# Expert products of a transformer layer: 256 weight columns per matmul in place of 512

## The chip, the core and the metric

The kernel runs on one core of a Trainium2 chip. The metric is the device time of one execution in microseconds (us); less is better. The core has a matmul engine (PE, with its weight loads shown apart as PEld), three engines for elementwise work (DVE, ACT, POOL), a queue engine (SP), and 16 DMA engines. On PE one operand is stationary: a load (LDWEIGHTS) puts it into the array, and a matmul then streams the moving operand past it, column by column, into PSUM. The next load may run while a matmul streams.

## What is computed

A layer with three attention branches (differential attention, RWKV-7 time mixing, memory attention), a joint output projection, and a mixture of 16 experts, all in f32. 512 tokens of width 1024; each token goes to 2 of 16 experts of hidden width 512. The part that the change touches is the last loop:

```python
y = jnp.zeros_like(xt)
for e in range(N_EXPERTS):
    hdn = jax.nn.silu(xt @ w_gate[e]) * (xt @ w_up[e])
    y = y + gate[:, e:e + 1].astype(xt.dtype) * (hdn @ w_down[e])
return y.reshape(B, S, D)
```

## The kernel before

Each expert gets a table of up to 96 token slots (`CAP`). Its rows are gathered from memory (`gather`), turned on PE against an identity (`turn_x`), and split into a high and a low part (`xh`, `xl`, f32r). The expert's weights stream in by pieces of 128 partitions x 1024 columns, 512 KB each, 12 pieces an expert (4 of gate, 4 of up, 4 of down), issued by SP. For each piece `WeightStream.pump` makes a high part on ACT (`whi`, L96) and a low part on DVE (`wlo`, L97); there are four pairs of these tiles, and a pair comes free (`ws.cool`) when the products that read it have run.

A product keeps f32 accuracy with three matmuls (`mm3`, L242 to L245): high x high, high x low, low x high. In an expert the activations are the stationary operand (128 partitions x 96 columns) and the weights are the moving one (128 x 512). `in_product` (gate, then up) runs 8 slices of the contraction x 3 matmuls into one PSUM bank (`pp`); `down` runs 4 slices x 2 halves of the output x 3 matmuls into two banks (`py`; for the last expert two `pp`). That is 24 + 24 + 24 = 72 matmuls an expert and 1152 in all. Between the products of an expert stand the turns of the next expert's rows (`turn_x`, L1280, 8 matmuls) and of the hidden rows (`turn_h`, L1302, 4 matmuls), and the table of a later expert (`table`, L1223, 4 small matmuls).

The order of the instructions on each engine is made ahead of the run by a scheduler that has its own estimate of what each takes. So a change in the form of the matmuls can move others around them, on all engines.

Two earlier stages use matmuls of 256 moving columns, with 128 stationary columns: the projections (mm3 on `w_in` and `w_kv`) and the output projection (`out_part`, L998 to L1000):

```python
T.matmul(o, ah, hi[:, k % 4, :], start=k == k0 and i == lead, stop=False, skip_group_check=True)
T.matmul(o, ah, lo[:, k % 4, :], start=False, stop=False, skip_group_check=True)
T.matmul(o, al, hi[:, k % 4, :], start=False, stop=k == k1, skip_group_check=True)
```

Of the kernel before, what the change touches and what calls it, by code (L numbers as in the profile page):

```python
# [24 lines left out]
KC = D // P  # L25
# [3 lines left out]
CAP = 96  # L29
# [121 lines left out]
def hybrid_layer_kernel(ctx, tc, x, mem, positions, cols, w_in, w_kv, w_out, wa2, g2, ffn, wr, br,  # L151
                        wg, wu, wd, out):
    nc = tc.nc
    V, A, G, T = nc.vector, nc.scalar, nc.gpsimd, nc.tensor
# [16 lines left out]
    def pp():  # L171
        return psp.tile([P, 512], F32, name="pp", bufs=4)
# [69 lines left out]
    def mm3(ps, ah, al, bh, bl, first, last):  # L242
        T.matmul(ps, ah, bh, start=first, stop=False)  # L243
        T.matmul(ps, ah, bl, start=False, stop=False)  # L244
        T.matmul(ps, al, bh, start=False, stop=last)  # L245

    def paired(steps):

        before = steps[0]()
        for step in steps[1:]:  # L250
            with tc.issue_after(before.ins):
                before = step()

    def rsqrt(pool, ss, n, mul, epsv, tag, wide=False):
        v = pool.tile([P, n], F32, name="rs_v" + tag)
        y = pool.tile([P, n], F32, name="rs_y" + tag)
        t = pool.tile([P, n], F32, name="rs_t" + tag)
        V.tensor_scalar(v, ss, mul, epsv, op0=ALU.mult, op1=ALU.add)
        if wide:
            G.tensor_tensor(y, v, mhalf.to_broadcast([P, n]), op=ALU.pow)  # L260
        else:
            A.activation(t, v, AF.Ln)
            A.activation(y, t, AF.Exp, scale=-0.5)
        V.tensor_mul(t, y, y)
        V.scalar_tensor_tensor(t, t, -0.5, v, op0=ALU.mult, op1=ALU.mult)
        V.scalar_tensor_tensor(y, t, 1.5, y, op0=ALU.add, op1=ALU.mult)
        return y
# [256 lines left out]
    def rwkv():  # L524
# [4 lines left out]
        with tc.manual_schedule(engines={mybir.EngineType.Activation}):  # L529
            A.activation(th[0:64, :], lor[0:64, 0, :], AF.Tanh)  # L530
            A.activation(th[64:128, :], lor[64:128, 0, :], AF.Copy)
            A.activation(sg, lor[:, 1, :], AF.Sigmoid)
            yield 1.8
            f0 = b4("f0", [P, 4 * S + 2 * NCH])
            f1 = bR("f1", [P, 2, 2, S])
            f2 = bR("f2", [P, 2, 2, S])
            pc_ = f0[:, 0:2 * S + 2 * NCH].rearrange("p (j c t) -> p j c t", j=2, t=C + 1)
            sw = f0[:, 2 * S + 2 * NCH:].rearrange("p (j t) -> p j t", j=2)
            cs, kk, sq, ip = f1[:, 1], f2[:, 0], f2[:, 1], f1[:, 1]
            aa = f1[:, 0]  # L540
            V.memset(pc_[:, :, :, 0], 1.0)
            for j in range(2):
                pw = [pc() for _ in range(2)]
                paired([lambda o=o: T.matmul(pw[o], wa2_sb[sr(o), j * P:(j + 1) * P], th[sr(o), :], start=True, stop=True)
                        for o in range(2)])
                for dst, nb, ps in ((sw, 0, pw[0]), (aa, 2, pw[1])):
                    A.activation(dst[:, j, :], ps, AF.Sigmoid, bias=col[:, C_W0 + nb + j:C_W0 + nb + j + 1])
                V.tensor_tensor_scan(cs[:, j, :], rmask, sw[:, j, :], 0.0, op0=ALU.mult, op1=ALU.add)
                yield 2.0
            A.preload_act_table_set("natural_log_exp_and_others")  # L550
            A.activation(pc_[:, :, :, 1:], cs.rearrange("p j (c t) -> p j c t", t=C), AF.Exp, scale=-KAPPA)
            A.activation(ip, cs, AF.Exp, scale=KAPPA)
# [59 lines left out]
        for ci in range(4):  # L612
            pq = [pc() for _ in range(2)]
            paired([lambda h=h, q=q: T.matmul(pq[q][:, h * P:(h + 1) * P], bk[sr(q), ci, h], u1[sr(q), q, ci, h],
                                              start=True, stop=True) for h in range(4) for q in range(2)])
            for q in range(2):
                pv = pq[q].rearrange("p (h n) -> p h n", h=4)
                A.activation(u2[sr(q), ci, :, 0:64], pv[sr(q), :, 0:64], AF.Copy)
                V.tensor_mul(u2[sr(q), ci, :, 64:128], pv[sr(q), :, 64:128],
                             gm[sr(q), None, 64:128].to_broadcast([64, 4, 64]))  # L620
                V.tensor_mul(u1[vr(q), q, ci], pv[vr(q)], gm[vr(q), None, :].to_broadcast([64, 4, P]))
                yield 1.0
# [79 lines left out]
        def inverse(q):  # L702
            ra = slice(q * 64, q * 64 + 32)
            rb = slice(q * 64 + 32, q * 64 + 64)
            ps = pc()
            for i in range(16):
                T.matmul(ps[rb, i * 32:(i + 1) * 32], u2v[ra, i, 32:64], zt[ra, i, 0:32], start=True, stop=True)
            A.activation(qt[rb].rearrange("p u n -> p (u n)"), ps[rb, :], AF.Copy)
            yield 2.0
            ps = pc()  # L710
            for i in range(16):
                T.matmul(ps[rb, i * 32:(i + 1) * 32], u2v[rb, i, 32:64], qt[rb, i, :], start=True, stop=True)
            A.activation(zt[rb, :, 0:32], ps[rb, :].rearrange("p (u n) -> p u n", n=32), AF.Copy)
            yield 2.0
            for g in range(2):
                ps = pc()
                ps2 = pc()

                def merge(i, second):
                    ci, h = divmod(g * 8 + i, 4)  # L720
                    zl = zt[sr(q), g * 8 + i, :]
                    if second:
                        return T.matmul(ps2[vr(q), i * C:(i + 1) * C], zl, u2[sr(q), ci, h, 64:128], start=True, stop=True)
                    return T.matmul(ps[sr(q), i * C:(i + 1) * C], zl, bkt[sr(q), q * 4 + ci, h, :], start=True, stop=True)
                paired([lambda i=i, z=z: merge(i, z) for i in range(8) for z in (False, True)])
                A.activation(bkt[sr(q), q * 4 + g * 2:q * 4 + g * 2 + 2].rearrange("p c h n -> p (c h) n"),
                             ps[sr(q), :].rearrange("p (u n) -> p u n", n=C), AF.Copy)
                A.activation(u2v[sr(q), g * 8:g * 8 + 8, 64:128], ps2[vr(q), :].rearrange("p (u n) -> p u n", n=C),
                             AF.Copy)
                yield 2.0  # L730
# [301 lines left out]
    def pl(n):  # L1032
        return pools["ps"].tile([P, 96], F32, name="pl", bufs=2)[:, 0:n]
# [139 lines left out]
    def step(t, n=1):  # L1173
        for _ in range(n):
            next(turns[t])
# [107 lines left out]
    def in_product(xh, xl):  # L1283
        ps = pp()
        for b in range(4):
            hi, lo = ws.use()
            for k in range(2):
                kk_ = b * 2 + k
                mm3(ps[0:CAP, :], xh[:, kk_, :], xl[:, kk_, :], hi[:, k, :], lo[:, k, :], kk_ == 0, kk_ == KC - 1)
            ws.cool(1)  # L1290
        return ps

# [21 lines left out]
    def down(hh, hl, si, gs, last=False):  # L1314
        py = [pp(), pp()] if last else pools["ps"].tile([P, 2, 512], F32, name="py", bufs=1)
        for k in range(4):
            hi, lo = ws.use()
            for n in range(2):
                ns = slice(n * 512, (n + 1) * 512)
                mm3(py[n][0:CAP, :] if last else py[0:CAP, n, :], hh[:, k, :], hl[:, k, :], hi[:, 0, ns], lo[:, 0, ns], k == 0, k == 3)  # L1320
            ws.cool(1)
        ye = ex_p.tile([CAP, D], F32, name="ye", bufs=3)
        if last:
            A.activation(ye[:, 0:512], py[0][0:CAP, :], AF.Copy, scale=gs)
            V.tensor_scalar(ye[:, 512:D], py[1][0:CAP, :], gs, None, op0=ALU.mult)
        else:
            A.activation(ye, py[0:CAP].rearrange("p a b -> p (a b)"), AF.Copy, scale=gs)
        G.indirect_dma_start(out, bass.IndirectOffsetOnAxis(ap=si, axis=0), ye, None, compute_op=ALU.add)  # L1328
# [17 lines left out]
    for e in range(NE):  # L1346
        pg = in_product(*xt_)
        if e + LEAD < NE and e + LEAD > 3:
            with tc.issue_after(last_x[-1].ins):
                table(e + LEAD, e + LEAD + 1)()  # L1350
            xg.append(gather(gidx[0:CAP, e + LEAD:e + LEAD + 1]))
        hs = turn_h(sl) if sl is not None else None
        xt2 = turn_x(xg[e + 1]) if e + 1 < NE else None
        pu = in_product(*xt_)
        sl = hidden(pg, pu)
        xt_ = xt2
        if hs:
            down(*hs, sidx[0:CAP, e - 1:e], gslot[0:CAP, e - 1:e])
# [12 lines left out]
    with tc.If(full > CAP):  # L1371
        with tc.For_i(0, NE, 1) as e:
# [5 lines left out]
            for b in range(1, (S + CAP - 1) // CAP):  # L1378
                base = ex_p.tile([P, CAP], F32, name="base")
                V.tensor_scalar(base, slot1, float(b * CAP), None, op0=ALU.add)  # L1380
                ps = pl(96)
# [56 lines left out]
```

## Time and profile before

| what | us |
|---|---|
| time, median of 3 runs (lowest, highest) | 634.29 (633.48, 638.74) |
| the profiled execution: its time | 633.17 |
| its span from first to last instruction | 631.4 |
| PE busy in the span | 600.7 |
| DVE, ACT, POOL busy | 498.0, 413.0, 126.3 |
| expert stage, about | from 335 to 619 |

The profile shows one execution. A matmul's duration in it is a model that holds its pipeline too, so that durations of matmuls that follow each other overlap; what a matmul costs in a dense stretch is the step from its start to the start of the next. The same is true of loads. Some matmul records are missing from the trace (3986 of 4021 are there).

### The profile page before, as it was taken

Reading aid. Unit: us, or ns where it says so; the run is one execution under the profiler, and the core shown is the slowest. Engines: PE = TensorE matmul, PEld = TensorE weight load, DVE = VectorE, ACT = ScalarE, POOL = GpSimd, SP = SyncE. Lnnn points to the kernel's source line nnn. Section 1 sums busy time; section 2 is a strip of 40 time slices with the busy share of each in tenths; the row PEclk is TensorE's granted clock in tenths of the full one; section 3 lists DMA queues with packets and bytes.
Section 4 is the critical chain, followed back from the end, with each engine's and each line's share of the span. In section 5 each row is a group of like instructions: output and inputs, shape, how many; then the busy total and the mean of one; then the engine's idle time right before and its main releaser. Section 6 shows DMA issues by size and latency. Waiting matters only on the chain.

```text
span 631.4 us, 10888 instructions
## 1 busy us (share of the span) xinstructions
PE 600.7 (95%) x3986; PEld 482.1 (76%) x3986; DVE 498.0 (79%) x893; ACT 413.0 (65%) x622; POOL 126.3 (20%) x129
## 2 busy tenths in 40 slices
PE   3899999999999999999998999999999999999992
PEld 3777879999998877889996777777777777777771
DVE  5854996699755778555468999999999999988991
ACT  3677344544367766655247788888889888888880
POOL 6802010335400114304001011111011111310001
PEclk9999989999999999999999999999999999999997
DMA  8523233333432030889789999999999999799813
GB/s 304 158 79 87 80 102 83 101 95 108 103 83 68 2 134 1 292 278 344 274 315 310 354 348 370 369 372 356 360 357 363 364 366 373 227 379 374 320 25 54
DMA packets 77501, 144.17 MB, mean 228 GB/s; under 512 B 12832, under 2 KB 30496, under 8 KB 77440
## 3 DMA queue, kind: packets, MB, share of 16 engines
q1 hardware_dynamic: 69200, 126.07, 56.9%
q0 software_dynamic: 3760, 13.24, 8.9%
q10 hardware_dynamic: 4480, 4.09, 2.1%
q8 instruction: 33, 0.54, 0.4%
q14 instruction: 28, 0.23, 0.1%
HBM read 131.72 MB, written 11.67 MB: 227 GB/s over the span
## 4 chain that ended last, share of the span: by engine, by line
PE 86%; DVE 6%; ACT 3%; DMA 2%; issue 1%; POOL 1%; POOLq 0%; ACTq 0%; DVEq 0%
PE pp L243 16%; PE pp L245 16%; PE pp L244 16%; PE py L244 5%; PE py L245 4%; PE py L243 4%; PE pp L998 2%; PE pp L999 2%; PE pp L1000 2%; PE pt L921 2%; PE pp L1280 1%; PE py L1136 1%; PE pc L781 1%; DVE wlo L97 1%; PE pl L1103 1%
## 5 line engine op out<-in xcount | busy, mean ns | idle before, releaser
L245 PE MATMUL pp<-whi,xl 128*96 128x512 f32 x264 | 104.0, 395 | 0.0
L244 PE MATMUL pp<-wlo,xh 128*96 128x512 f32 x264 | 103.8, 394 | 0.0
L243 PE MATMUL pp<-whi,xh 128*96 128x512 f32 x264 | 101.2, 394 | 0.8 <-ACT xh L1267 0.8
L1328 POOL DMA_INDIRECT out<-ye,sidx x16 | 23.2, 1452 | 226.0 <-DVE gidx L1230 90.7
L97 DVE TENSOR_TENSOR wlo<-raw,whi 128x1024 fp32r<-128x1024 f32 x42 | 52.3, 1258 | 15.5 <-ACT whi L96 15.0
L96 ACT ACTIVATE whi<-raw 128x1024 fp32r<-128x1024 f32 x42 | 44.1, 1059 | 31.2 <-PE pp L245 14.0
L243 PE MATMUL pp<-whi,hm_h 128*128 128x256 f32 x224 | 63.5, 284 | 0.1
L245 PE MATMUL pp<-whi,hm_l 128*128 128x256 f32 x224 | 63.3, 283 | 0.0
L244 PE MATMUL pp<-wlo,hm_h 128*128 128x256 f32 x224 | 63.1, 282 | 0.0
L243 PEld LDWEIGHTS pp<-whi,xh 128*96 128x96 f32 x264 | 42.5, 161 | 19.6 <-ACT xh L1267 1.3
L245 PEld LDWEIGHTS pp<-whi,xl 128*96 128x96 f32 x264 | 42.6, 161 | 18.4
L244 PEld LDWEIGHTS pp<-wlo,xh 128*96 128x96 f32 x264 | 42.5, 161 | 18.2
L244 PE MATMUL py<-wlo,hh 128*96 128x512 f32 x120 | 47.9, 399 | 0.0
L245 PE MATMUL py<-whi,hl 128*96 128x512 f32 x120 | 47.1, 392 | 0.0
L243 PE MATMUL py<-whi,hh 128*96 128x512 f32 x120 | 47.0, 392 | 0.0
L97 DVE TENSOR_TENSOR wlo<-u,whi 128x1024 fp32r<-128x1024 f32 x34 | 40.8, 1224 | 6.3 <-ACT whi L96 6.3
L97 DVE TENSOR_TENSOR wlo<-lraw,whi 128x1024 fp32r<-128x1024 f32 x36 | 42.6, 1218 | 2.8 <-ACT whi L96 2.7
L243 PEld LDWEIGHTS pp<-whi,hm_h 128*128 128x128 f32 x224 | 42.0, 188 | 2.0 <-issue 0.7
L245 PEld LDWEIGHTS pp<-whi,hm_l 128*128 128x128 f32 x224 | 42.1, 188 | 0.6 <-issue 0.2
L244 PEld LDWEIGHTS pp<-wlo,hm_h 128*128 128x128 f32 x224 | 42.1, 188 | 0.5 <-issue 0.2
L96 ACT ACTIVATE whi<-lraw 128x1024 fp32r<-128x1024 f32 x36 | 37.1, 1059 | 5.1 <-PE pp L245 3.6
L96 ACT ACTIVATE whi<-u 128x1024 fp32r<-128x1024 f32 x34 | 35.2, 1058 | 6.7 <-PE pp L1000 3.7
(397 smaller groups left out, 1545.5 us busy)
## 6 DMA issues: line engine op xcount, KB each, us to landing
raw<-in_w_in SPq DMA_DIRECT2D x22, 512.0 KB, 3.8
u<-in_wd SPq DMA_DIRECT2D x12, 512.0 KB, 7.3
lraw<-in_wg SPq DMA_DIRECT2D x12, 512.0 KB, 11.7
lraw<-in_wu SPq DMA_DIRECT2D x12, 512.0 KB, 9.3
lraw<-in_wd SPq DMA_DIRECT2D x12, 512.0 KB, 12.5
f<-in_wg SPq DMA_DIRECT2D x11, 512.0 KB, 10.3
u<-in_wu SPq DMA_DIRECT2D x11, 512.0 KB, 12.5
eraw<-in_wd SPq DMA_DIRECT2D x10, 512.0 KB, 13.4
```

The costliest lines, as they stand in the source:

```text
L96: nc.scalar.activation(hi, slot, AF.Copy)
L97: nc.vector.tensor_sub(lo, slot, hi.bitcast(F32))
L243: T.matmul(ps, ah, bh, start=first, stop=False)
L244: T.matmul(ps, ah, bl, start=False, stop=False)
L245: T.matmul(ps, al, bh, start=False, stop=last)
L781: T.matmul(px[:, h * C:(h + 1) * C], u1[:, q, ci, h], sav[:, c, h, :], start=h == 0, stop=True, skip_group_check=True)
L921: T.matmul(po[:, 0:P], aws[i % 2][:, kb * P:(kb + 1) * P], qk["v"][:, kb, h * P:(h + 1) * P], start=kb == 0, stop=kb == qb)
L998: T.matmul(o, ah, hi[:, k % 4, :], start=k == k0 and i == lead, stop=False, skip_group_check=True)
L999: T.matmul(o, ah, lo[:, k % 4, :], start=False, stop=False, skip_group_check=True)
L1000: T.matmul(o, al, hi[:, k % 4, :], start=False, stop=k == k1, skip_group_check=True)
L1103: T.matmul(pr_[:, 0:20], xT[:, k, :], wr_sb[:, k, :], start=k == 0, stop=k == KC - 1)
L1328: G.indirect_dma_start(out, bass.IndirectOffsetOnAxis(ap=si, axis=0), ye, None, compute_op=ALU.add)
```

## The change

The three matmuls of a slice become six: each is cut into two with half of the moving columns (256), into the two halves of the same PSUM bank. The stationary operand of both is the same. In the first slice only the first of the six has the start flag.

```diff
+    def mm3_halves(ps, ah, al, bh, bl, first, last):
+        for z, (a, b) in enumerate(((ah, bh), (ah, bl), (al, bh))):
+            for n in range(2):
+                c = slice(n * 256, n * 256 + 256)
+                T.matmul(ps[:, c], a, b[:, c], start=first and z + n == 0, stop=last and z == 2, skip_group_check=True)
...
-                mm3(ps[0:CAP, :], xh[:, kk_, :], xl[:, kk_, :], hi[:, k, :], lo[:, k, :], kk_ == 0, kk_ == KC - 1)
+                mm3_halves(ps[0:CAP, :], xh[:, kk_, :], xl[:, kk_, :], hi[:, k, :], lo[:, k, :], kk_ == 0, kk_ == KC - 1)
...
-                mm3(py[n][0:CAP, :] if last else py[0:CAP, n, :], hh[:, k, :], hl[:, k, :], hi[:, 0, ns], lo[:, 0, ns], k == 0, k == 3)
+                mm3_halves(py[n][0:CAP, :] if last else py[0:CAP, n, :], hh[:, k, :], hl[:, k, :], hi[:, 0, ns], lo[:, 0, ns], k == 0, k == 3)
```

Lines behind the new function stand 6 further down in the kernel after: L1302 is L1308 there, and the matmuls of L243 to L245 are at L258.

PE, in the middle of an expert, before: the last slice of a down product (`py`) begins, one product of the next matrix (`pp`) follows, then the turns (L1302, L1280) and the four matmuls of a table (L1223, with their loads), and the down product goes on.

```order
L243 MATMUL py_4686<-whi3_87,hh_4626 96x512
L243 MATMUL pp_4726<-whi0_80,xh_4640 96x512
L1302 MATMUL pp_4783<-ident_104,sl_4683 128x96 x4
L1280 MATMUL pp_4792<-ident_104,xg_4457 128x96 x4
L1280 MATMUL pp_4793<-ident_104,xg_4457 128x96 x4
L1223 LDWEIGHTS ohs_4764
L1223 MATMUL pl_4763<-rhs_3188,ohs_4764 96x6
...
L1223 LDWEIGHTS ohs_4773
L1223 MATMUL pl_4763<-rhs_3188,ohs_4773 96x6
L244 MATMUL py_4686<-wlo3_88,hh_4626 96x512
```

The same place after:

```order
L258 MATMUL py_5070<-whi3_87,hh_4986 96x256 x2
L258 MATMUL pp_5134<-whi0_80,xh_5000 96x256 x2
L1308 MATMUL pp_5215<-ident_104,sl_5067 128x96 x4
L1286 MATMUL pp_5224<-ident_104,xg_4745 128x96 x4
L1229 LDWEIGHTS ohs_5196
...
L1286 MATMUL pp_5225<-ident_104,xg_4745 128x96
L1229 LDWEIGHTS ohs_5202
L1229 MATMUL pl_5195<-rhs_3188,ohs_5202 96x6
L1286 MATMUL pp_5225<-ident_104,xg_4745 128x96
...
L1286 MATMUL pp_5225<-ident_104,xg_4745 128x96 x2
L258 MATMUL py_5070<-wlo3_88,hh_4986 96x256 x2
```

Each 96x512 row has become two rows of 96x256, and the four table matmuls, which stood together, now stand between the turns in three groups; the order of the products around them is the same.

PE at the end of the program, before: the down product of expert 14 (`py`), with the turn of the last expert's hidden rows (L1302) behind the first product of its third weight piece (`whi2`), and then the last expert's down product (`pp`).

```order
L243 MATMUL py_6201<-whi2_85,hh_6161 96x512
L1302 MATMUL pp_6237<-ident_104,sl_6198 128x96 x4
L244 MATMUL py_6201<-wlo2_86,hh_6161 96x512
...
L243 MATMUL py_6201<-whi3_87,hh_6161 96x512
...
L245 MATMUL py_6201<-whi3_87,hl_6162 96x512
L243 MATMUL pp_6246<-whi0_80,xh_6242 96x512
```

The same place after:

```order
L258 MATMUL py_7305<-whi2_85,hl_7242 96x256 x2
L258 MATMUL py_7305<-whi3_87,hh_7241 96x256 x2
L1308 MATMUL pp_7365<-ident_104,sl_7302 128x96 x4
L258 MATMUL py_7305<-wlo3_88,hh_7241 96x256 x2
...
L258 MATMUL py_7305<-whi3_87,hl_7242 96x256 x2
L258 MATMUL pp_7374<-whi0_80,xh_7370 96x256 x2
L258 MATMUL pp_7374<-wlo0_81,xh_7370 96x256 x2
L258 MATMUL pp_7375<-whi0_80,xh_7370 96x256 x2
```

The turn has moved back by six products, behind the first product of the fourth weight piece; five products are left between it and the last expert's down product, where eleven were. On ACT the copy that takes the turned rows out of PSUM (L1310, L1316 after) has moved back by two weight pieces:

```order
L96 ACTIVATE whi3_87<-raw0_79 128x1024
L96 ACTIVATE whi0_80<-raw1_82 128x1024
L1310 ACTIVATE xh_6242<-pp_6237 128x384
L96 ACTIVATE whi1_83<-u2_2365 128x1024
L96 ACTIVATE whi2_85<-u2_2365 128x1024
L1327 ACTIVATE ye_6234<-py_6201,gslot_3717 96x1024
```

and after:

```order
L96 ACTIVATE whi3_87<-raw0_79 128x1024
L96 ACTIVATE whi0_80<-raw1_82 128x1024
L96 ACTIVATE whi1_83<-u2_2365 128x1024
L96 ACTIVATE whi2_85<-u2_2365 128x1024
L1316 ACTIVATE xh_7370<-pp_7365 128x384
L1333 ACTIVATE ye_7362<-py_7305,gslot_3717 96x1024
```

The low part of the same rows on DVE (`xl`, L1311) has moved behind the same two pieces' `wlo`.

## Rows read from the trace of the kernel before

**Rows 1.** The page's first part: busy us (share of the span) xinstructions of each engine.

```profile
PE 600.7 (95%) x3986; PEld 482.1 (76%) x3986; DVE 498.0 (79%) x893; ACT 413.0 (65%) x622; POOL 126.3 (20%) x129
```

**Rows 2.** Windows, expert stage: length, busy us by engine, PE clock, DMA share, GB/s.

```profile
352.00:440.00 88.00, 88.00 (x438) 63.12 (x437) 82.80 (x128) 71.99 (x84) 12.04 (x10) 1.00 1.05 359
440.00:530.00 90.00, 90.00 (x445) 64.47 (x444) 85.65 (x126) 74.62 (x87) 12.69 (x11) 1.00 1.05 367
```

**Rows 3.** Waits, 360 to 600 us: who for whom, us in total, times, longest.

```profile
DVE wlo L97 <- ACT whi L96: 13.2, 27, 1.4
ACT whi L96 <- PE pp L245: 10.3, 24, 0.5
```

**Rows 4.** Groups by form, whole span: xcount | busy us, mean ns | idle before.

```profile
L245 PE MATMUL pp<-whi,xl 128*96 128x512 f32 x264 | 104.0, 395 | 0.0
L245 PE MATMUL py<-whi,hl 128*96 128x512 f32 x120 | 47.1, 392 | 0.0
L244 PEld LDWEIGHTS pp<-wlo,xh 128*96 128x96 f32 x264 | 42.5, 161 | 18.2
L243 PEld LDWEIGHTS pp<-whi,xh 128*96 128x96 f32 x264 | 42.5, 161 | 19.6 <-ACT xh L1267 1.3
L998 PEld LDWEIGHTS pp<-xhi,hm_h 128*128 128x128 f32 x32 | 6.0, 188 | 0.0
```

**Rows 5.** Timeline of PE, a gate product: start us, us, instruction.

```profile
420.20 0.39 PE L244 MATMUL pp<-wlo,xh 128*96 128x512 f32 x1
...
425.76 0.39 PE L244 MATMUL pp<-wlo,xh 128*96 128x512 f32 x1
```

**Rows 6.** Timeline of PE, a down product.

```profile
431.09 0.39 PE L243 MATMUL py<-whi,hh 128*96 128x512 f32 x1
...
434.52 0.40 PE L243 MATMUL py<-whi,hh 128*96 128x512 f32 x1
```

**Rows 7.** Timeline of PE, the output projection, 256 moving columns.

```profile
288.00 0.28 PE L998 MATMUL pp<-xhi,hm_h 128*128 128x256 f32 x1
...
290.72 0.28 PE L998 MATMUL pp<-whi,hm_h 128*128 128x256 f32 x1
```

**Rows 8.** Timeline of PE, the projection of the memory, 256 moving columns.

```profile
74.50 0.28 PE L245 MATMUL pp<-whi,qT 128*128 128x256 f32 x1
...
75.58 0.28 PE L245 MATMUL pp<-whi,qT 128*128 128x256 f32 x1
```

**Rows 9.** Windows of rows 8, 7 and 5.

```profile
74.50:75.60 1.10, 1.10 (x12) 1.10 (x10) 1.07 (x2) 0.00 (x0) 0.00 (x0) 1.00 0.00 0
288.00:290.70 2.70, 2.70 (x26) 2.70 (x25) 2.70 (x4) 2.70 (x6) 1.94 (x2) 1.00 1.03 407
420.20:425.76 5.56, 5.56 (x25) 3.87 (x24) 4.88 (x11) 5.05 (x6) 2.43 (x2) 1.00 1.04 397
```

**Rows 10.** Timeline of PE, a table between the turns and the products.

```profile
435.98 0.30 PE L1223 MATMUL pl<-rhs,ohs 128*96 128x6 bf16 x4
436.14 0.45 PE L244 MATMUL py<-wlo,hh 128*96 128x512 f32 x1
436.43 0.40 PE L245 MATMUL py<-whi,hl 128*96 128x512 f32 x1
```

**Rows 11.** Timeline of PE, ACT and DVE, 610 to 616 us.

```profile
610.67 0.49 PE L1302 MATMUL pp<-ident,sl 96*128 96x96 f32 x4
...
613.52 0.62 PE L243 MATMUL pp<-whi,xh 128*96 128x512 f32 x2
...
611.20 0.49 ACT L1310 ACTIVATE xh<-pp 128x384 fp32r<-128x384 f32 x1 [0.87 <-PE pp L1302]
611.59 2.00 ACT L96 ACTIVATE whi<-u 128x1024 fp32r<-128x1024 f32 x2
...
612.14 0.55 DVE L1311 TENSOR_TENSOR xl<-pp,xh 128x384 fp32r<-128x384 f32 x1
612.67 2.36 DVE L97 TENSOR_TENSOR wlo<-u,whi 128x1024 fp32r<-128x1024 f32 x2
```

## The prediction

> **What bounds the kernel now.** I read the engines' busy shares first. PE is busy 95% of the span, and each matmul has its own load: 3986 of the one, 3986 of the other [rows 1]. Then the windows of the expert stage: PE is busy for 88.00 of 88.00 us and 90.00 of 90.00, at the full granted clock (1.00), with DVE next at 82.80 and 85.65 [rows 2]. So PE is never without a matmul there, and DVE has some 5% to spare. The waits agree: DVE waits for ACT's high parts (13.2 us) and ACT waits for PE to give weight tiles back (10.3 us) [rows 3]; the products' own groups show 0.0 us idle before them [rows 4]. Everything that feeds the experts is ahead of PE, so what PE takes for the 1152 products goes into the time one for one.
>
> A product's price is its step, from one start to the next, and not its 392 to 395 ns of duration [rows 4], which holds the pipeline. In a gate product 24 steps take 425.76 - 420.20 = 5.56 us: 231.7 ns each [rows 5]. In a down product 15 steps take 434.52 - 431.09 = 3.43 us: 228.7 ns [rows 6]. Of the 1152 products 264 x 3 = 792 are written into `pp` and 120 x 3 = 360 into `py` [rows 4], so they take 792 x 231.7 + 360 x 228.7 ns = 183.5 + 82.3 = 265.8 us of the 633.17 of this execution. (It lies 1.1 us under the median of 634.29; the sums below are against 633.17.)
>
> **The change, part by part.** It removes 1152 steps of 512 columns and puts in 2304 of 256. Nothing else is added but the load that comes with each matmul: the trace gives no sign that a load is left out where the stationary operand stays, since high x high and high x low use the same one, and both have 264 loads [rows 4].
>
> *The new step.* No row has 256 moving columns beside 96 stationary ones, so I bound it by the two rows with 256 moving and 128 stationary. In the output projection 24 steps take 290.72 - 288.00 = 2.72 us: 113.3 ns [rows 7]. In the memory's projection 9 steps take 75.58 - 74.50 = 1.08 us: 120.0 ns [rows 8]. The granted clock is 1.00 in both, and the load of the other engines does not explain the two levels: the cheap one has DMA at 1.03 and all of DVE and ACT busy, as the experts have (1.04), and the dear one has DMA at 0.00 [rows 9]. So both levels can occur in the experts, and what chooses between them is not in the profile. By the low one all 2304 steps take 261.0 us, 4.8 less than now: two cheap halves (226.7 ns) are shorter than one product of today. By the high one they take 276.5 us, 10.7 more.
>
> Where in between? Today's products stand 231.7 - 226.7 = 5.0 ns (`pp`) and 2.0 ns (`py`) above two cheap halves, though all have one shape. If that surplus belongs to a load running beside a stream, it is paid once a load, and the split pays it twice: +792 x 5.0 + 360 x 2.0 ns = +4.7 us. If it belongs to the long stream it goes away: -4.8 us. I take the middle of the two rows, 116.7 ns, which is 268.8 us, **+3.0 us**; it is nearer to the surplus per load, because a load here is over well before a 512 stream ends (161 ns in 232) and still costs it something. The ends of the range keep both levels.
>
> *The loads' own time.* A load of 96 columns shows 161 ns [rows 4], and the experts' load row is busy 63.12 of 88.00 us [rows 2]. Doubled that is 126 of 88. But the loads of 128 columns show 188 ns [rows 4] and come every 113.3 ns with the row busy 2.70 of 2.70 us [rows 7, 9]: they overlap, and the duration is no occupancy. I cost it at nothing beyond the step.
>
> The Trainium skill, in "Perfetto Trace Analysis", section "Identifying the Most-Contended Engine", says that the busy share of LDWEIGHTS and not that of the matmuls tells how much room the engine has. By that the loads would need 1.4 times the stage and become the bound, some 100 us more. Row 7's pitch, under a load's duration, speaks against reading it so here.
>
> *The table between the turns.* The four bf16 matmuls now stand in up to three groups, two groups more for each of some 11 experts. One return from them to f32 costs 436.43 - 436.14 = 0.29 us where a product's step is 0.23 [rows 10]: 0.06 us. So 22 x 0.06 = 1.3 us at most, and nothing if the turns don't pay it; I take **+0.5**.
>
> *The end.* The turn of the last hidden rows goes from 610.67 to six products later: 610.67 + 6 x 0.229 = 612.04, and is out at about 612.4. Its ACT copy (0.49 us) then stands behind two weight pieces (2.00 us for both). The second of them needs `whi2` back, which PE frees about one product ahead of the turn, at 611.8; so it runs to 612.9 and the copy to 613.4, just ahead of the last expert's first product (613.52). On DVE the low part (0.55 us) stands behind that piece's `wlo` (2.36 us for two, 1.18 each): 612.9 + 1.18 + 0.55 = 614.6, and PE wants it at the fifth product, 613.52 + 4 x 0.229 = 614.44 [rows 11]. So about 0.2 us are lost, 0.5 at most, 0 if all is early; behind the copy on ACT stand the scaling of expert 14's output and the last weight piece, which PE wants three pieces later. I take **+0.3**.
>
> No wait is added elsewhere. If PE gains, as by the low level, DVE's 82.80 of 88.00 us become 82.80 of 86.4: still under the span.
>
> Sum: 633.17 + 3.0 + 0.5 + 0.3 = **637.0 us**, 0.6% over its own execution.
>
> **Rivals.**
>
> *The high level holds* (120 ns, as in rows 8): 633.17 + 10.7 + 0.8 = 644.7. For it: a stationary operand and a stream that meet so do it at every step of a whole product. Against: half of today's evidence, and the nearer stage by load, is at the low one. From 117.8 ns on the change is slower by more than 1%. Chance 0.27.
>
> *The low level holds*, or the chip leaves the second load out, so that the change adds no load at all: 113.3 ns, 633.17 - 4.8 + 0 to 0.8 = 628.4 to 629.2, faster by 0.7%. For it: row 7, the same streams at the same DMA load. Against: the surplus of rows 5. From 114.3 ns down (263.3 us, -2.5) I count it here. Chance 0.20; a quarter of it with a step under 112 ns (smaller load, 96 columns for 128), which would be faster by over 1%.
>
> *The load, or whatever hands PE its instructions, becomes the bound*: at 161 ns a load 2304 x 161 ns = 371 us, +105: 738. Against it: rows 7. Chance 0.03.
>
> **How the numbers follow.** The forecast, steps between 114.3 and 117.8 ns, 633.17 - 2.5 to + 6.3, has 0.50. Then low 0.20, high 0.27, bound by loads 0.03. About 1% (6.3 us) is what a measurement of this kernel tells from no change. Faster by over 1%: 0.05. Slower by over 1%: 0.27 + 0.03 = 0.30. Within 1%: 0.65. The range goes from the low level, 628.4, to the high one with all its extras, 633.17 + 10.7 + 1.3 + 0.5 = 645.7; it leaves out the loads as the bound, and the ends of the outer cases, some 0.15 in all. The forecast's own range is 630.7 to 639.5.
>
> **What would show it.** In the trace after: 2304 products at 256 columns, each with its load; the step over a run of them, 116.7 by the forecast, and whether `pp` and `py` differ in it; PE busy all of the expert stage and no idle before products; loads that show about 161 ns and overlap; at the end a gap before the fifth product of the last expert. The distance from one expert's turns to the next then grows by some 0.2 us. It would be wrong if PE waited for ACT or DVE in the expert stage, or if loads came no closer than their duration.

## The result and the profile after

The median over 21 runs is 638.69 us, against 634.53 us for the kernel before; the ratio is 1.0057, with a 95% interval of 1.0040 to 1.0073. The ratio is formed over the fast executions alone and is not the quotient of these two medians. The forecast was 637.0 us, or +0.6%: the time lies in its range, and it moved the way that was said.

The profiled execution took 647.04 us, more than the median. In it PE's granted clock was 0.50, the level of 1.2 GHz, from 204 to 223 us, in the attention stage, which the change doesn't touch. PE was busy throughout the 14 us before that, at 0.96, and the 19 us at half the clock cost up to 9.5 us, about what this execution stands above the median (8.4). What follows is read from the expert stage, where the clock is 1.00 in both kernels. Page part 1 and windows of the kernel after (length, busy us of PE, PEld, DVE, ACT, POOL, clock, DMA share, GB/s):

```profile
PE 615.8 (95%) x5138; PEld 576.6 (89%) x5138; DVE 499.1 (77%) x893; ACT 413.3 (64%) x622; POOL 123.3 (19%) x129
```

```profile
190.00:204.00 14.00, 14.00 (x174) 12.41 (x173) 5.44 (x18) 9.52 (x22) 0.00 (x0) 0.96 0.22 68
204.00:223.00 19.00, 19.00 (x112) 15.17 (x111) 9.45 (x36) 7.69 (x25) 1.62 (x2) 0.50 0.03 9
366.00:454.00 88.00, 88.00 (x780) 88.00 (x779) 82.34 (x123) 71.60 (x83) 12.63 (x11) 1.00 1.04 356
454.00:544.00 90.00, 90.00 (x796) 90.00 (x795) 84.25 (x125) 73.27 (x85) 11.84 (x10) 1.00 1.04 363
```

There are 1152 matmuls and 1152 loads more than in [rows 1]: every half has its own load, though its stationary operand is that of the half before. PE is busy all of the expert stage, as in [rows 2]. The row of the loads went from 63.12 of 88.00 us to 88.00 of 88.00. From the start of the first expert product to the end of the last go 619.17 - 332.07 = 287.10 us before (the first pair of lines) and 634.30 - 342.35 = 291.95 after. So the stage grew by 4.85 us, less than 2%, and not by the 40% that reading the row as occupancy would ask for.

```profile
332.07 0.48 PE L243 MATMUL pp<-whi,xh 128*96 128x512 f32 x1 [0.44 <-ACT xh L1267]
...
618.78 0.39 PE L245 MATMUL pp<-whi,xl 128*96 128x512 f32 x1
```

```profile
342.35 0.48 PE L258 MATMUL pp<-whi,xh 128*96 128x256 f32 x2 [0.44 <-ACT xh L1273]
...
633.90 0.40 PE L258 MATMUL pp<-whi,xl 128*96 128x256 f32 x2
```

The chain that ended last, in order of time (start us, us, what), now shows runs of products in one piece:

```profile
431.11 9.85 PE pp L258 x84
442.37 4.22 PE py L258 x36
```

9.85 us over 84 steps is 117.3 ns, 4.22 over 36 is 117.2. Two halves take 234.6 ns, where a whole product took 231.7 in [rows 5] and 228.7 in [rows 6]. The groups show the same durations per load as [rows 4], and, in the group shown, no wait before the products (us, mean ns, idle before):

```profile
L258 PE MATMUL pp<-wlo,xh 128*96 128x256 f32 x528 | 105.0, 280 | 0.0
L258 PEld LDWEIGHTS pp<-wlo,xh 128*96 128x96 f32 x528 | 73.6, 161 | 0.0
```

At the end of the program the wait that the prediction looked for is there. The timelines of PE, of ACT and of DVE:

```profile
628.81 0.40 PE L258 MATMUL pp<-wlo,xh 128*96 128x256 f32 x2
629.37 0.71 PE L258 MATMUL pp<-whi,xl 128*96 128x256 f32 x4 [0.17 <-DVE xl L1317]
```

```profile
627.49 0.47 ACT L1316 ACTIVATE xh<-pp 128x384 fp32r<-128x384 f32 x1
```

```profile
628.77 0.55 DVE L1317 TENSOR_TENSOR xl<-pp,xh 128x384 fp32r<-128x384 f32 x1
```

The two products at 628.81 should be followed after 0.23 us; the next one, which is the first to read `xl`, comes after 0.56, when DVE has finished it at 628.77 + 0.55 = 629.32. So 0.33 us are lost here.

### The profile page after: what moved, and what is told of

It reads as the page before. It is cut to its first block, busy times and chain, and to the rows that moved or that the text cites. A ratio compares the mean times of both kernels' runs of the same rounds, so it can differ in the third digit from the quotient of the medians.

```text
span 645.3 us, 13190 instructions
## 1 busy us (share of the span) xinstructions
PE 615.8 (95%) x5138; PEld 576.6 (89%) x5138; DVE 499.1 (77%) x893; ACT 413.3 (64%) x622; POOL 123.3 (19%) x129
## 4 chain that ended last, share of the span: by engine, by line
PE 86%; DVE 6%; ACT 3%; issue 2%; POOL 1%; DMA 1%; POOLq 0%; ACTq 0%; DVEq 0%
PE pp L258 28%; PE py L258 13%; PE pp L243 7%; PE pp L244 7%; PE pp L245 7%; PE pp L1004 2%; PE pp L1005 2%; PE pp L1006 2%; PE pt L927 2%; PE pp L1286 2%; DVE wlo L97 1%; PE pc L787 1%; PE py L1142 1%; PE pl L1109 1%; PE pc L620 1%
## 5 line engine op out<-in xcount | busy, mean ns | idle before, releaser
L258 PE MATMUL pp<-wlo,xh 128*96 128x256 f32 x528 | 105.0, 280 | 0.0
L258 PE MATMUL pp<-whi,xl 128*96 128x256 f32 x528 | 104.7, 279 | 0.2 <-DVE xl L1317 0.2
L258 PE MATMUL pp<-whi,xh 128*96 128x256 f32 x528 | 102.9, 280 | 0.8 <-ACT xh L1273 0.8
L258 PEld LDWEIGHTS pp<-whi,xl 128*96 128x96 f32 x528 | 73.8, 162 | 0.5 <-DVE xl L1317 0.4
L258 PEld LDWEIGHTS pp<-whi,xh 128*96 128x96 f32 x528 | 72.7, 161 | 1.1 <-ACT xh L1273 1.1
L258 PEld LDWEIGHTS pp<-wlo,xh 128*96 128x96 f32 x528 | 73.6, 161 | 0.0
L243 PE MATMUL pp<-whi,hm_h 128*128 128x256 f32 x224 | 63.5, 284 | 0.1
L245 PE MATMUL pp<-whi,hm_l 128*128 128x256 f32 x224 | 63.3, 283 | 0.0
L258 PE MATMUL py<-wlo,hh 128*96 128x256 f32 x240 | 48.5, 283 | 0.0
L258 PE MATMUL py<-whi,hh 128*96 128x256 f32 x240 | 47.7, 280 | 0.0
L258 PE MATMUL py<-whi,hl 128*96 128x256 f32 x240 | 47.6, 279 | 0.0
L243 PEld LDWEIGHTS pp<-whi,hm_h 128*128 128x128 f32 x224 | 42.0, 188 | 2.0 <-issue 0.7
L245 PEld LDWEIGHTS pp<-whi,hm_l 128*128 128x128 f32 x224 | 42.1, 188 | 0.6 <-issue 0.2
```

The source lines that it names most:

```text
L258: T.matmul(ps[:, c], a, b[:, c], start=first and z + n == 0, stop=last and z == 2, skip_group_check=True)
```

## The experiments

All of them compute the whole layer. Each ratio is to the kernel before, measured on the same chip beside it, and stands with its 95% interval.

**1 and 2: one kind of product alone.** In the first only the gate and up products are cut, in the second only the down products.

The edit of experiment 1:

```diff
-                mm3_halves(py[n][0:CAP, :] if last else py[0:CAP, n, :], hh[:, k, :], hl[:, k, :], hi[:, 0, ns], lo[:, 0, ns], k == 0, k == 3)
+                mm3(py[n][0:CAP, :] if last else py[0:CAP, n, :], hh[:, k, :], hl[:, k, :], hi[:, 0, ns], lo[:, 0, ns], k == 0, k == 3)
```

The edit of experiment 2:

```diff
-                mm3_halves(ps[0:CAP, :], xh[:, kk_, :], xl[:, kk_, :], hi[:, k, :], lo[:, k, :], kk_ == 0, kk_ == KC - 1)
+                mm3(ps[0:CAP, :], xh[:, kk_, :], xl[:, kk_, :], hi[:, k, :], lo[:, k, :], kk_ == 0, kk_ == KC - 1)
```

> Only the gate and up products (768 of 1152) are cut in halves; the down products stay whole. Steps of the halves 117 ns as with all products cut, steps of the whole down products 228.7 ns as before. By the theory that the step alone makes the difference: 768 x (2 x 117.3 - 231.7 ns) = +2.2 us over the kernel before, ratio about 1.003, and with the run that cuts the down products alone it adds up to the 3.6 us of the whole change. By the rival that the moved turns and tables make it, the steps would not explain the time and the two parts would not add up.

> Only the down products (384 of 1152) are cut; gate and up stay whole. By a surplus paid once a load and kept by kind of product (2.0 ns a load for the down products), halves of 115.3 ns and 384 x 2.0 ns = +0.8 us, ratio 1.001. By a surplus that is the same for every half, 117.2 ns: 384 x (234.4 - 228.7) = +2.2 us, ratio 1.003.

Measured: 1.0033 (1.0008 to 1.0057) and 1.0036 (1.0005 to 1.0066). The chain of experiment 1, then of experiment 2:

```profile
405.20 9.85 PE pp L258 x84
```

```profile
415.07 4.24 PE py L258 x36
```

These are 117.3 and 117.8 ns a step. The halves cost the same in both kinds, though the whole products they replace did not; so the surplus is not one that a kind of product carries along from the whole to its halves. The two parts add to +0.69%, which with their intervals agrees with the +0.57% of the whole change. The steps alone explain 768 x 2.9 = 2.2 us and 384 x 6 = 2.3 us, and +0.33% and +0.36% of 634 us are 2.1 and 2.3.

**3: quarters.** Where does a load become the bound?

```diff
-            for n in range(2):
-                c = slice(n * 256, n * 256 + 256)
+            for n in range(4):
+                c = slice(n * 128, n * 128 + 128)
```

> Every product cut in four of 128 columns. If a load sets a floor under the step: 128-column loads before short streams come every 112 ns in the trace of before, their shown duration is 188 ns against 161 ns at 96 columns, so the floor at 96 columns is about 112 - 27 = 85 ns, 4608 x 85 = 392 us against 270 us in halves, about 755 to 760 us in all. If there is no floor and each quarter takes its stream and the same surplus, 56.7 + 3.9 = 60.6 ns, 279 us, about 647 us. If the load's shown duration were its occupancy, 161 ns, 742 us for the products, above 1100 us in all.

Measured: 781.31 us, ratio 1.229 (1.2235 to 1.2348). Its chain, a wait and the matmul that ended it:

```profile
476.71 8.16 PE py L258 x96
```

```profile
PE pp L258 <- ACT sl L1301: 10.9, 13, 1.0
```

```profile
468.34 0.56 PE L258 MATMUL pp<-whi,xh 128*96 128x128 f32 x4 [0.82 <-ACT sl L1301]
```

8.16 us over 96 steps is 85.0 ns, as the floor by loads said ahead of the run. The products take 4608 x 85.0 = 391.7 us. The time is some 23 us above what I expected, in part because PE now also stands still: the 13 waits of the row alone are 10.9 us, behind the turns, for an operation on ACT. The rest is not accounted for. So halves (117 ns) are above the floor, and quarters (61 ns by their stream) under it.

That the floor goes with the load, and not with the stream, is borne out by the kernel before, where eight matmuls with 128 stationary columns and a stream of only 20 follow each other (a line of PE's timeline, and durations in ns, least, median and most):

```profile
302.21 1.05 PE L1103 MATMUL pl<-wr_sb,xT 128*128 128x20 f32 x8
```

```profile
L1103 PE MATMUL pl<-wr_sb,xT x64: 180/266/266, 293.9 to 324.9; 128*128 128x20 f32 x64
```

Without the 0.27 us of the last one, seven steps take 0.78 us, some 112 ns each. 112 to 85.0 is 1.32, and 128 to 96 columns of the load is 1.33.

**4: the same change with the tiles 32 bytes further.** What chooses between the two levels of [rows 7] and [rows 8]? The guess is the distance of the two operands of a matmul: how far apart their places in a partition are, modulo 128 bytes. In the built program the weight tiles begin 32 bytes past a multiple of 128 in a partition. The stationary tiles of the output projection are at a distance of 64 bytes from them, those of the memory projection at 0, and those of the experts at 32. An unused tile in the experts' pool moves the last:

```diff
     xt_ = split_x([first_py[:, b, :] for b in range(2)])
+    ex_p.tile([P, 8], F32, name="shift")
```

> The kernel after with one unused tile of 32 bytes a partition more in the experts' pool, which moves the activations (xh, xl, hh, hl) and the landing tiles down by 32 bytes; the order of all instructions is the same. The activations then lie 64 bytes from the weight tiles modulo 128, where they lay 32 (output projection, steps of 113.3 ns: 64; memory projection, 120.0 ns: 0). By the theory that this distance sets the surplus: steps of 113.3 ns in place of 117.2, 2304 x 3.9 ns = 9.0 us less than after, ratio to before about 0.992. By the rival that the surplus comes from the traffic of the stage or from the width of the load: 117.2 ns as before, ratio 1.006.

Measured: 0.9939 (0.9910 to 0.9969), so 1.2% less than the kernel after, and less than the kernel before. Its chain and a window:

```profile
399.99 9.54 PE pp L258 x84
410.89 4.08 PE py L258 x36
```

```profile
434.00:524.00 90.00, 90.00 (x822) 90.00 (x821) 86.79 (x129) 74.79 (x87) 12.13 (x10) 1.00 1.05 362
```

113.6 and 113.3 ns: the level of [rows 7], with every instruction in the order of the kernel after. PE is still busy for all of the window, and DVE, at 86.79 of 90.00, still follows.

**5 and 6: whole products, moved.** The same tile, of 32 and of 96 bytes, in the kernel before: distances of 64 and of 0.

> The kernel before (products whole, 512 columns) with the same 32-byte tile: the same order, activations 64 bytes from the weights modulo 128. By the theory that this distance sets the surplus for whole products too: steps of 226.7 ns in place of 231.0, 1152 x 4.3 ns = 5.0 us less, ratio 0.992, and the cut is worth nothing once the tiles lie well. The only whole products that lie 64 apart so far (first projections, 128 stationary columns) stand at about 229 ns; by them 2.3 us less, ratio 0.996. By the rival that placement matters for halves alone: 231 ns, ratio 1.000.

> The kernel before with a 96-byte tile: activations at the same place as the weights modulo 128 (distance 0, as in the memory projection, whose halves take 120.0 ns, 6.7 above 113.3). If the surplus is paid once a load: whole products of 226.7 + 6.7 = 233.3 ns, +2.7 us, ratio 1.004. If it is paid along the whole stream: 240 ns, +10.4 us, ratio 1.016.

Measured: 1.0018 (0.9998 to 1.0039) and 0.9995 (0.9969 to 1.0022). PE in a gate product, 24 steps, of experiment 5 and of experiment 6:

```profile
440.12 0.40 PE L244 MATMUL pp<-wlo,xh 128*96 128x512 f32 x1
...
445.69 0.39 PE L244 MATMUL pp<-wlo,xh 128*96 128x512 f32 x1
```

```profile
424.12 0.39 PE L243 MATMUL pp<-whi,xh 128*96 128x512 f32 x1
...
429.69 0.39 PE L243 MATMUL pp<-whi,xh 128*96 128x512 f32 x1
```

Both are 5.57 us for 24 steps, 232.1 ns, as in [rows 5]. So the theory that the distance sets the surplus of whole products in the same way fell, by both runs. They are not indifferent to the place, though. In experiment 5 a down product takes 435.91 - 432.44 = 3.47 us for 15 steps, 231.3 ns, where 15 took 3.43 us, 228.7 ns, at a distance of 32 [rows 6]:

```profile
432.44 0.39 PE L243 MATMUL py<-whi,hh 128*96 128x512 f32 x1
...
435.91 0.39 PE L243 MATMUL py<-whi,hh 128*96 128x512 f32 x1
```

At 64, where halves turn out low, whole products are not shorter, and those of the down kind are a little longer.

**7 and 8: halves at the other distances.** The kernel after with a tile of 96 bytes (distance 0) and of 64 bytes (32, on the other side).

> The kernel after with a 96-byte tile: distance 0. By the placement theory steps of 120.0 ns, 2304 x (120.0 - 117.3) = +6.2 us over the kernel after, ratio to before 1.0155; with the 32-byte tile (113.5 ns) it gives both ends of the range of the prediction in one kernel. By the rival that the 32-byte tile helped by the new place of the landing tiles: 117 ns or less, ratio at most 1.006.

> The kernel after with a 64-byte tile: distance 32 again, now on the other side, while all tiles of the pool have moved. By the placement theory 117 ns and a ratio of 1.006, as without the tile. If it is the move itself or the landing tiles: something else.

Measured: 1.0070 (1.0039 to 1.0102) and 1.0079 (1.0057 to 1.0101). Their chains:

```profile
408.02 9.87 PE pp L258 x84
419.30 4.22 PE py L258 x36
```

```profile
420.22 9.88 PE pp L258 x84
431.53 4.25 PE py L258 x36
```

These are 117.2 to 118.1 ns a step. Moving the tiles does nothing in itself, which answers the rival of experiment 4. But distance 0 is not the high level here: the 120.0 ns of the memory projection did not come, and 7 missed its 1.0155. What is left is that a distance of 64 is low, and that 0 and 32 to either side are alike.

**9 and 10: the weights moved in place of the activations.** A tile of 32 bytes ahead of the weight tiles: the experts come to a distance of 64 by the other way, and the first projections and the output projection leave it, for 32.

```diff
     ring = ctx.enter_context(tc.tile_pool(name="ring", bufs=1))
+    ring.tile([P, 8], F32, name="shift")
```

> The kernel after, but now the weight tiles (and all that is allocated behind them on that side) are moved up by an unused tile of 32 bytes, and the experts' activations stay. Order of the instructions unchanged. Weights and activations of the experts are 64 bytes apart modulo 128 by this other way; the output projection and the first projections, which were 64 apart (113.3 to 114.3 ns), are now 32 apart; the memory projection stays at 0. If the distance of 64 is the cause of the low step: experts 113.5 ns (-8.7 us against the kernel after), the 1056 steps of 256 columns in the projections up to about 117 ns (+2.9 us), together a ratio of about 0.997. If it was something else about the 32-byte tile in the experts' pool: experts 117.3, ratio 1.006. A third case: the weights now begin on a multiple of 64 bytes where they began 32 beside it; if a stream pays for a begun piece of 64 bytes, steps fall below 113 ns, towards 256 columns at 2.4 GHz = 106.7 ns, up to 15 us less.

> The kernel before (products whole) with the weights moved in the same way. By the finding that whole products don't respond to the distance: 231 ns, and the projections at about 117 ns as beside it: +2.9 us, ratio 1.004. If a stream that begins on a multiple of 64 bytes is cheaper in itself, whole products gain too: below 227 ns, ratio 0.995 or less.

Measured: 1.0023 (0.9998 to 1.0048) with halves and 1.0068 (1.0042 to 1.0094) with whole products. The chain of experiment 9 in the expert stage, and PE in its output projection (21 steps):

```profile
407.25 9.52 PE pp L259 x84
418.12 4.08 PE py L259 x36
```

```profile
293.57 0.28 PE L1005 MATMUL pp<-xhi,hm_h 128*128 128x256 f32 x1
...
296.06 0.28 PE L1005 MATMUL pp<-xhi,hm_h 128*128 128x256 f32 x1
```

The experts step at 113.3 ns and the output projection, at 113.3 in [rows 7], now at 2.49 us / 21 = 118.6. Both went the way that the distance says, in one program and in opposite directions. The third case fell: a stream that begins on a multiple of 64 bytes is not cheaper by itself. The projections lost more than the 2.9 us that I had put down, so 9 ends at 1.0023 and not at 0.997. A step went to 118.6 ns in this stretch, where I had put 117, and I had left out the 192 whole products of the first projections (128 stationary, 512 moving columns). They answer to the distance too. 21 of their steps take 4.81 us before, at 64 (229.0 ns), and 4.90 us in experiment 10, at 32 (233.3 ns), which is 0.8 us for all of them:

```profile
60.50 0.39 PE L243 MATMUL pp<-hm_h,whi 128*128 128x512 f32 x1
...
65.31 0.40 PE L244 MATMUL pp<-hm_l,whi 128*128 128x512 f32 x1
```

```profile
61.16 0.40 PE L244 MATMUL pp<-hm_h,whi 128*128 128x512 f32 x1
...
66.06 0.40 PE L245 MATMUL pp<-hm_l,whi 128*128 128x512 f32 x1
```

Run 10, where nothing is gained in the experts, shows that loss alone: +0.68%, 4.3 us; 0.9939 + 0.0068 = 1.0007 lies in the interval of 9. The experts of 10 are nearly as before. The token turns of two experts in a row, in the timeline of PE of the kernel before and then of experiment 10, are 17.85 and 17.89 us apart:

```profile
435.32 0.82 PE L1280 MATMUL pp<-ident,xg 96*128 96x96 f32 x8
...
453.17 0.82 PE L1280 MATMUL pp<-ident,xg 96*128 96x96 f32 x8
```

```profile
423.25 0.82 PE L1281 MATMUL pp<-ident,xg 96*128 96x96 f32 x8
...
441.14 0.82 PE L1281 MATMUL pp<-ident,xg 96*128 96x96 f32 x8
```

## Why the prediction held

**What bounds.** Right: PE was without a gap in the windows of the expert stage before and is so after, and the stage grew by about what the steps grew by. The waits of ACT for PE and of DVE for ACT in that stage are of the size of [rows 3]:

```profile
DVE wlo L97 <- ACT whi L96: 14.4, 32, 1.4
ACT whi L96 <- PE pp L258: 12.0, 26, 0.6
```

**The step.** 116.7 ns was taken as the middle of 113.3 and 120.0, and 117.3 was measured: 2304 x 117.3 = 270.3 us, +4.4 in place of +3.0. Bounding from the rows was sound. That the step came out so near the middle was luck: the experts' tiles happened to lie at a distance of 32, which neither row had, and at 64, as in [rows 7], the same cut takes 113.3 ns. One reason given for the middle was not sound: a surplus paid once a load and kept by kind would have made 113.3 + 5.0 = 118.3 ns in the gate and up products and 113.3 + 2.0 = 115.3 in the down products, and experiments 1 and 2 show 117.3 and 117.8. Its sum, +4.7, came out near by chance. The real choice between the levels was one that the prediction said is "not in the profile": experiments 4, 7, 8 and 9 show it to hang on where the two operands lie. The low rival was thus live, and comes true with 32 bytes more of memory (0.9939, with an interval of 0.9910 to 0.9969; the rival's 628.4 to 629.2 us are 0.9925 to 0.9937 of its 633.17). The high one did not come at any place tried: in the stretches read, the experts took 118.1 ns at most.

**The loads.** It is right that 161 ns is no occupancy; the floor of a load is 85.0 ns (experiment 3), under a half's stream and over a quarter's.

**The table.** Priced at +0.5, at most 1.3. The turn ahead of [rows 10] in the kernel before, and then the same place in the kernel after (timelines of PE):

```profile
434.99 0.49 PE L1302 MATMUL pp<-ident,sl 96*128 96x96 f32 x4
```

```profile
446.66 0.49 PE L1308 MATMUL pp<-ident,sl 96*128 96x96 f32 x4
...
447.83 0.45 PE L258 MATMUL py<-wlo,hh 128*96 128x256 f32 x2
448.13 0.40 PE L258 MATMUL py<-whi,hl 128*96 128x256 f32 x2
```

From the turn to the first down product go 436.14 - 434.99 = 1.15 us before and 1.17 after, and the return to the products still costs 0.30 for two halves where 0.23 is the rule. So about 0.02 an expert by this place, 0.2 us in all: nearly nothing, for here too the products pay the return from bf16 once, however the groups stand.

**The end.** +0.3 predicted, 0.33 seen, and at the product that was named, the first that reads `xl`.

Together that is 4.4 + 0.2 + 0.3 = 4.9 us by this profile, against 3.8 predicted. It agrees with the 4.85 us by which the stage grew in these two executions. The ratio gives 3.6 us (2.5 to 4.6); why it reads about a microsecond less is not shown.

**Still open.** Why a distance of 64 bytes gives the low step to halves and does not shorten the whole products of an expert; why 0 gives a steady 120.0 ns with 128 stationary columns and 117.5 with 96; and the surplus of whole products, which stayed near 232 ns in a gate product at all three places tried. Only distances in multiples of 32 bytes were tried, and no run looked inside a step.

## What to carry to other kernels

Where PE is the bound and never waits, price an edit of its matmuls by the step from start to start in a dense stretch of the same trace, not by the shown durations of matmuls and loads, and look for a stretch with the same number of columns; this kernel had two in other stages. If such stretches show two levels for one shape, try the placement of the operands before settling on a shape: here the same cut is +0.6% as it lay, and with 32 unused bytes it is -0.6%, against +0.18% (-0.02 to +0.39%) for the whole products with the same tile. And before making a stream shorter, compare it with the floor of its load: halves stayed above it, and quarters, under it, cost 23%.

## What I had not expected of the hardware

- In this kernel the step of a matmul with 256 moving f32r columns hangs on the distance of its two operands modulo 128 bytes in their partitions: 113.3 to 113.6 ns at 64, 117.2 to 118.1 at 0 and at 32 to either side (96 stationary columns); 113.3 at 64, 118.6 at 32 and 120.0 at 0 (128 stationary columns).
- Two halves at the low level (226.6 ns) are shorter than one whole gate product (231.7), although they load the same stationary operand twice.
- With 96 stationary f32r columns on 128 partitions and streams of 128, a matmul steps at 85.0 ns, about half of the 161 ns that its load shows.
